# Three rounded products for mLSTM's scores, and moved loads and steps, in a two-layer trunk on one Trainium2 core

## The chip, the cores and the metric

The kernel runs on one core of a Trainium2 chip (trn2). The metric is device time in microseconds (us); the median of the runs counts. Before the change it is 1042.13 us (three runs, 1041.74 to 1042.76).

The engines are named as in the profile: PE is TensorE (matmuls; PEld is its loading of weights), DVE is VectorE, ACT is ScalarE, POOL is GpSimd, SP is SyncE. An engine's name with a q is its queue of instructions, from which it also issues DMAs.

## The reference

The trunk has two layers over 256 tokens of width 2048, all in float32. Layer 0 mixes with HGRN2 and RG-LRU side by side, layer 1 with mLSTM. Cut to what the change touches:

```python
hn = rmsnorm(h, o_norm)                      # layer 1
u = hn @ o_w_in
qk, v, og, z, ig, fg = split(u)              # fg, ig: 8 columns each, the gate columns
qk = silu(causal_conv(qk, c_conv_w, c_conv_b))
q, k = qk[..., :1024], qk[..., 1024:]        # 8 heads of 128
# per head, stabilised; wts holds the decays and gates, zero above the diagonal
sc = (q @ k.T) * wts
num = sc @ v ; den = sum(sc)
...
h = h + mix                                  # residual, in both layers
pl = rmsnorm(p[i] @ ple_w[i], ple_norm[i])   # embedding of the layer
h = h + sigmoid(h @ ple_gate_w[i]) * pl
```

## The kernel before

All large products are float32 products in three parts. `load_weights` (L120) loads 128 rows of weights as two tiles of 1024 columns, rounds each on ScalarE to `whi` (L132) and has VectorE subtract for the rest, `wlo` (L133). The activations are split in the same way into a high and a low part. A product is then hi x hi, hi x lo, lo x hi: L193, L194, L195 in `quarter_tok` (L182), 24 matmuls of 512 columns to a quarter (a fourth of the 2048 input rows, for two halves of the tokens), four quarters to a chunk of 512 output columns. The tiles `raw` have five buffers, `whi` and `wlo` four each. Results stand in PSUM tiles `mm` (three) and `mx` (three); the small products of the mixers use `mx` and `st`.

The small work of the mixers is written as generators. They sit in lanes, and `pump` (L75), once per quarter after its first twelve matmuls, takes one step of the first generator in each lane. A bare `yield` is thus a wait of one quarter. Work that goes from token-major to feature-major form makes a trip through DRAM (`across`, L449): VectorE transposes, GpSimd writes one DMA (L452) and reads it back with four (L455), and after `lag` quarters the next step uses what has landed. Within an engine the order is that of a scheduler, which weighs the written order, priorities and the availability it expects.

The places that the change touches:

- **Head.** `embed` (L272) multiplies the layer's input embedding with its weights, 48 products at L293. The first block's weights come in four pieces of 256 and two of 512 columns, the second block's first half in two pieces of 512. Two pieces go out on ScalarE's queue, all else on SyncE's. Nine full-precision warm-up products (L96) run before. L302 and L304 copy results out of PSUM.
- **Trips.** `feature_major` (L476) takes the gated HGRN2 output to feature-major form (scaling at L483, split at L146 and L147), with a lag of 5. `gated_mix` (L797) does so for the RG-LRU gate, with a lag of 6 for the first half and 5 for the second; L804 multiplies with the recurrence. RG-LRU's sigmoids are L775, its own products L151 to L153. L852 and L853 take the gate projection out of PSUM.
- **Residual.** The four tiles `hq` (512 KB each) are loaded back to back by GpSimd (L865) right after the last trip of layer 0; `out_proj` adds a chunk's product to each (L374). Two row loads for the embedding's gain (L322) follow once the mixer's memory is free; L329 reads them.
- **Gate columns.** Their weights `gr` (128 KB) are loaded by SyncE (L882) and scaled on VectorE to `wg` (L885); the gate sums use `wg` in small products (L896) from 467 us on.
- **Scores.** `mix` (L1011) treats two heads. For each head it multiplies keys and queries as full float32 products: the first 128 keys with 256 tokens (L1032), the other 128 keys with the last 128 tokens (L1033). L1018, L1019, L1023 and L1024 make the weights `wt` from the stabiliser, L1034 applies them, L1037 and L1038 split the result into `sh` and `sl`, and L1052 multiplies these with the values.

## Time and profile before

| | us |
|---|---|
| median of three runs | 1042.13 |
| the profiled execution's own time | 1042.44 |
| its span, first to last instruction | 1040.7 |
| TensorE busy (matmuls) | 1030.2 (99%) |
| VectorE busy | 730.4 (70%) |
| ScalarE busy | 601.7 (58%) |
| HBM traffic | 225 GB/s over the span |
| granted TensorE clock | 0.998 |

A row of the timeline gives the start, the duration, the engine and line, the operation with its tiles (out<-in), the shape, and how many like instructions were merged; in brackets stand the idle time of the engine before it and what ended that. A row of the waits gives who waited for whom, the sum, how often, and the longest. A row on DMA issues gives what is loaded, by which queue, how often, its size, and the time to landing. A matmul's row lasts from its start to its modelled end, which overlaps with the next one; the distance from start to start is what it costs.

### The profile page before, as it was taken

How to read it: one execution, taken by the hardware profiler on the slowest of the kernel's cores; microseconds unless marked ns; L12 is line 12 of the kernel's file. 1: busy time of each engine (PE TensorE's matmuls, PEld its weight loads, DVE VectorE, ACT ScalarE, POOL GpSimd, SP SyncE). 2: the span in 40 equal slices, each digit the busy share in tenths (PEclk: the TensorE clock that was granted, in tenths of full speed). 3: DMA queues.
4: the chain of work that ended last, by engine and by line, in shares of the span. 5: the costliest groups of instructions: out<-in, count | busy, mean ns of one | idle time of the engine just before them, and what ended most of it. 6: DMA issues, size and time to landing. Idle time of an engine off the chain costs nothing.

```text
span 1040.7 us, 14521 instructions
## 1 busy us (share of the span) xinstructions
PE 1030.2 (99%) x5278; PEld 854.7 (82%) x5278; DVE 730.4 (70%) x1101; ACT 601.7 (58%) x887; POOL 90.1 (9%) x171
## 2 busy tenths in 40 slices
PE   9999999999999999999999999999999999999996
PEld 7888888888888888888788788888888888888886
DVE  7858878969685775777569976555457777666675
ACT  7675555587974444565557765644445557344553
POOL 0111101001121211111021000000001110111000
PEclk9999999999999999999999999999999999999999
DMA  9977646567779877687587654455557778788552
GB/s 343 342 246 228 222 160 210 179 202 232 234 247 313 288 248 242 212 276 239 179 268 253 201 173 153 162 183 186 198 195 230 247 257 284 240 251 247 195 182 82
DMA packets 67752, 234.80 MB, mean 226 GB/s; under 512 B 8800, under 2 KB 10080, under 8 KB 67680
## 3 DMA queue, kind: packets, MB, share of 16 engines
q1 hardware_dynamic: 55728, 196.64, 56.9%
q0 software_dynamic: 11520, 36.71, 11.7%
q8 instruction: 41, 0.67, 0.3%
q10 hardware_dynamic: 432, 0.52, 0.1%
q14 instruction: 31, 0.25, 0.1%
HBM read 216.02 MB, written 17.83 MB: 225 GB/s over the span
## 4 chain that ended last, share of the span: by engine, by line
PE 91%; issue 4%; DMA 2%; ACT 1%; POOL 1%; DVE 0%; ACTq 0%; DVEq 0%; POOLq 0%; SPq 0%
PE mm L193 25%; PE mm L194 25%; PE mm L195 25%; PE mx L195 3%; PE mx L193 3%; PE mx L194 3%; PE mm L293 2%; DMA gr<-in_ogf_dram 1%; PE nu L1052 1%; DMA r<-dzb 1%; PE mm L1180 1%; PE mm L1179 1%; PE mm L1178 1%; DMA dzb<-w 1%; POOL r L455 1%
## 5 line engine op out<-in xcount | busy, mean ns | idle before, releaser
L133 DVE TENSOR_TENSOR wlo<-raw,whi 128x1024 fp32r<-128x1024 f32 (+2 forms) x365 | 437.7, 1207 | 228.7 <-ACT whi L132 215.9
L132 ACT CAST whi<-raw 128x1024 fp32r<-128x1024 f32 (+2 forms) x365 | 378.9, 1041 | 328.5 <-PE mm L195 260.0
L193 PE MATMUL mm<-whi,ahl 128*128 128x512 f32 x1216 | 475.6, 391 | 0.0
L194 PE MATMUL mm<-wlo,ahl 128*128 128x512 f32 x1216 | 473.8, 390 | 0.4 <-DVE wlo L133 0.4
L195 PE MATMUL mm<-whi,ahl 128*128 128x512 f32 x1216 | 473.3, 389 | 0.0
L193 PEld LDWEIGHTS mm<-whi,ahl 128*128 128x128 f32 x1216 | 228.3, 188 | 49.3 <-issue 1.2
L194 PEld LDWEIGHTS mm<-wlo,ahl 128*128 128x128 f32 x1216 | 228.3, 188 | 48.2 <-DVE wlo L133 2.0
L195 PEld LDWEIGHTS mm<-whi,ahl 128*128 128x128 f32 x1216 | 228.2, 188 | 47.8
L193 PE MATMUL mx<-whi,ahl 128*128 128x512 f32 x160 | 62.4, 390 | 0.0
L195 PE MATMUL mx<-whi,ahl 128*128 128x512 f32 x160 | 62.3, 389 | 0.0
L194 PE MATMUL mx<-wlo,ahl 128*128 128x512 f32 x160 | 62.3, 389 | 0.0
L195 PEld LDWEIGHTS mx<-whi,ahl 128*128 128x128 f32 x160 | 30.0, 188 | 6.3
L194 PEld LDWEIGHTS mx<-wlo,ahl 128*128 128x128 f32 x160 | 30.0, 188 | 6.3
L193 PEld LDWEIGHTS mx<-whi,ahl 128*128 128x128 f32 x160 | 30.0, 188 | 6.2
L452 POOL DMA_DIRECT2D ducn<-w x4 | 2.2, 560 | 221.4 <-DVE w L465 221.4
L944 DVE SCALAR_TENSOR_TENSOR qk<-xr,prm,qk 128x255 f32<-128x255 f32 (+2 forms) x48 | 20.3, 471 | 0.1
L147 DVE TENSOR_TENSOR ahl<-xr,ahl 128x512 fp32r<-128x512 f32 x24 | 16.3, 685 | 4.1 <-ACT ahl L146 4.0
L1179 PE MATMUL mm<-wlo,ahl 128*128 128x256 f32 x64 | 18.1, 283 | 0.0
L1180 PE MATMUL mm<-whi,ahl 128*128 128x256 f32 x64 | 18.1, 283 | 0.0
L1178 PE MATMUL mm<-whi,ahl 128*128 128x256 f32 x64 | 18.1, 283 | 0.0
L293 PE MATMUL mm<-whi,ahl 128*128 128x512 f32 x56 | 17.6, 391 | 0.0
L146 ACT CAST ahl<-xr 128x512 fp32r<-128x512 f32 x24 | 14.7, 612 | 4.0 <-DVE xr L804 3.9
(316 smaller groups left out, 811.6 us busy)
## 6 DMA issues: line engine op xcount, KB each, us to landing
raw<-in_ew_dram SPq DMA_DIRECT2D x64, 512.0 KB, 5.3
raw<-in_g_dram SPq DMA_DIRECT2D x56, 512.0 KB, 4.7
raw<-in_eo_dram SPq DMA_DIRECT2D x32, 512.0 KB, 6.0
raw<-in_oqk_dram SPq DMA_DIRECT2D x32, 512.0 KB, 4.8
raw<-in_ov_dram SPq DMA_DIRECT2D x32, 512.0 KB, 4.0
raw<-in_oog_dram SPq DMA_DIRECT2D x32, 512.0 KB, 3.9
raw<-in_oz_dram SPq DMA_DIRECT2D x32, 512.0 KB, 4.1
raw<-in_oo_dram SPq DMA_DIRECT2D x32, 512.0 KB, 4.9
```

Of the source, the lines that this page charges most:

```text
L132: last["act"] = s.copy(h, r).ins
L133: last["dve"] = v.tensor_tensor(out=l, in0=r, in1=h.bitcast(F32), op=ALU.subtract).ins
L146: (v.tensor_copy if name == "p0" else s.copy)(hi, src)
L147: v.tensor_tensor(out=lo, in0=src, in1=hi.bitcast(F32), op=ALU.subtract)
L193: te.matmul(ps[hf], xh, wh, start=(k == 0), stop=False)
L194: te.matmul(ps[hf], xh, wl, start=False, stop=False)
L195: last["pe"] = te.matmul(ps[hf], xl, wh, start=False, stop=(k == KT - 1)).ins
L293: last["pe"] = te.matmul(ps[hf], tokens(pact[x], k, hf), (hi, lo)[y][:, k * 512:(k + 1) * 512], start=(n == mine[0]), stop=(n == mine[-1]) ...
L944: v.scalar_tensor_tensor(dst[:, sh:T], pi[:, 0:T - sh], pc("ccw", k * 16 + n), dst[:, sh:T], op0=ALU.mult, op1=ALU.add)
L1178: te.matmul(ps[hf], xh, wh, start=(k == 0), stop=False)
L1179: te.matmul(ps[hf], xh, wl, start=False, stop=False)
L1180: last["pe"] = te.matmul(ps[hf], xl, wh, start=False, stop=(k == KT - 1)).ins
```

## The change

In the head, `load_weights` takes its queues in turn. The first block's pieces go out on ScalarE's and SyncE's queue alternately (three on each), and the second block comes as two loads of 1024 columns, like all later weights. The lag of the HGRN2 trips goes from 5 to 6 quarters, that of the second RG-LRU gate trip from 5 to 6. Only two residual tiles are loaded after the last trip; the third and fourth follow behind the trips of the first and second output chunks. The product that scales the gate columns is ordered behind the last weight subtraction written before it. The scores of the first 128 keys become three products of rounded parts; queries and those keys are split into parts one quarter ahead.

```diff
-    def load_weights(src, pieces=(1, 1), queues=8 * (sy,)):
+    def load_weights(src, pieces=(1, 1), queues=(sy,)):
...
-                queues[hf * 4 + c // n].dma_start(out=r, in_=src[:, hf * 1024 + c:hf * 1024 + c + n])
+                queues[c // n % len(queues)].dma_start(out=r, in_=src[:, hf * 1024 + c:hf * 1024 + c + n])
...
-            parts = load_weights(w[b], *((((4, 2), (s, s) + 6 * (sy,)) if head else ((2, 1),)) if first else ()))
+            parts = load_weights(w[b], *(((4, 2), (s, sy)) if head else ()))
...
-            r = yield from landed((u[:, 0], u[:, 1]), f"dzb{j}", 6 - j)
+            r = yield from landed((u[:, 0], u[:, 1]), f"dzb{j}", 6)
...
-                start(f"fm{g}", feature_major(u, "an", 4 * g, y, 5))
+                start(f"fm{g}", feature_major(u, "an", 4 * g, y, 6))
...
-    for i in range(4):
+
+    def load_hq(i, behind):
         t = hp.tile([P, 2, 512], F32, name="hq", tag="h")
-        with tc.issue_after(last["hop"]):
+        with tc.issue_after(behind):
             gp.dma_start(out=t, in_=a["x"].rearrange("(h p) f -> p h f", h=2)[:, :, i * 512:(i + 1) * 512])
         hq.append(t)
 
+    for i in range(2):
+        load_hq(i, last["hop"])
+
     def mixed():
         for c, ps in enumerate(chunks(a["eo"], 4, y, ready(y, "fm"))):
+            if c in (1, 2):
+                load_hq(c + 1, last["hop"])
...
-    v.tensor_tensor(out=wt[:, :, 0:16], in0=gr, in1=pall("on").unsqueeze(2).to_broadcast([P, KT, 16]), op=ALU.mult)
+    with tc.issue_after(last["dve"]):
+        v.tensor_tensor(out=wt[:, :, 0:16], in0=gr, in1=pall("on").unsqueeze(2).to_broadcast([P, KT, 16]), op=ALU.mult)
...
+        def room2(which):
+            return bp.tile([P, 1024], F32R, name=which, tag="wt")
+
...
             yield
-            yield
             while 4 + j not in qk:
                 yield
+            qhl = room2("qhl").rearrange("p (s i t) -> p s i t", s=2, i=2)
+            khl = tp.tile([P, 512], F32R, name="khl", tag="th").rearrange("p (s i t) -> p s i t", s=2, i=2)
+            for hl, src in ((qhl, qk[j].rearrange("p (i t) -> p i t", i=2)),
+                            (khl, qk[4 + j].rearrange("p (i t) -> p i t", i=2)[:, :, 0:P])):
+                s.copy(hl[:, 0], src)
+                v.tensor_tensor(out=hl[:, 1], in0=src, in1=hl[:, 0].bitcast(F32), op=ALU.subtract)
+            yield
             for i in range(2):
                 q, k = qk[j][:, i * T:(i + 1) * T], qk[4 + j][:, i * T:(i + 1) * T]
                 sc = px.tile([P, 512], F32, name="mx", tag="mx")
-                te.matmul(sc[:, 0:T], k[:, 0:P], q, start=True, stop=True)
+                for n, (x, z) in enumerate(((0, 0), (0, 1), (1, 0))):
+                    te.matmul(sc[:, 0:T], khl[:, x, i], qhl[:, z, i], start=(n == 0), stop=(n == 2))
                 te.matmul(sc[:, T:384], k[:, P:T], q[:, P:T], start=True, stop=True)
```

Three places show what moves in the engines' order. Line numbers in rows of the change are those of the changed kernel, 6 to 17 higher from L804 on. First VectorE around the gate columns' product, at 320 to 345 us; L133 is a weight subtraction, L804 and L147 make the last activations of the output projection, L329 reads the row loads, L374 adds the residual. Before:

```order
L133 TENSOR_TENSOR wlo<-raw,whi 128x1024 x4
L804 TENSOR_TENSOR xr<-r,tt 128x512 x2
L147 TENSOR_TENSOR ahl<-xr,ahl 128x2x256 x2
L133 TENSOR_TENSOR wlo<-raw,whi 128x1024 x2
L885 TENSOR_TENSOR wg<-gr,prm 128x16x16
L133 TENSOR_TENSOR wlo<-raw,whi 128x1024 x4
L329 TENSOR_TENSOR pl<-pl,row 128x512
L374 TENSOR_TENSOR hq<-mm,hq 128x512
```

And in the change:

```order
L133 TENSOR_TENSOR wlo<-raw,whi 128x1024 x6
L804 TENSOR_TENSOR xr<-r,tt 128x512 x2
L147 TENSOR_TENSOR ahl<-xr,ahl 128x2x256 x2
L133 TENSOR_TENSOR wlo<-raw,whi 128x1024 x4
L329 TENSOR_TENSOR pl<-pl,row 128x512
L374 TENSOR_TENSOR hq<-mm,hq 128x512
```

The product of the gate columns has left this place (it stands 56 instructions later), and L804 comes two subtractions later. Second, ScalarE ahead of the gate projection's way out of PSUM (L852, L853), at 280 to 293 us; L483 is the scaling of the second HGRN2 trip, L132 a weight cast, L782, L787 and L790 belong to RG-LRU. Before:

```order
L787 ACTIVATE sq<-av 128x512
L782 ACTIVATE av<-av,spm_242 128x256
L483 ACTIVATE xr<-r,prm 128x256
L787 ACTIVATE sq<-av 128x512
L852 ACTIVATE th<-mm,rth 128x512
L853 ACTIVATE u<-mm,rcr 128x512
```

And in the change:

```order
L787 ACTIVATE sq<-av 128x512
L782 ACTIVATE av<-av,spm_239 128x256
L787 ACTIVATE sq<-av 128x512
L852 ACTIVATE th<-mm,rth 128x512
L853 ACTIVATE u<-mm,rcr 128x512
L852 ACTIVATE th<-mm,rth 128x512
L853 ACTIVATE u<-mm,rcr 128x512
L790 ACT_TABLE_LOAD
L790 ACTIVATE tt<-tt 128x1024
L132 CAST whi<-raw 128x1024 x3
L483 ACTIVATE xr<-r,prm 128x256
```

The scaling has moved behind both pairs of copies, the square root and three casts. Third, VectorE ahead of the first score weighting (L1034 before, L1051 now), at 597 to 606 us; L944, now L951, is a tap of the convolution of the last queries and keys, L948, now L955, closes it. Before:

```order
L944 SCALAR_TENSOR_TENSOR qk<-xr,prm,qk 128x255 x2
L948 SCALAR_TENSOR_TENSOR qk<-th,qk 128x512
L944 SCALAR_TENSOR_TENSOR qk<-xr,prm,qk 128x254 x2
L944 SCALAR_TENSOR_TENSOR qk<-xr,prm,qk 128x253
L133 TENSOR_TENSOR wlo<-raw,whi 128x1024 x2
L944 SCALAR_TENSOR_TENSOR qk<-xr,prm,qk 128x253
L1034 SCALAR_TENSOR_TENSOR wt<-mx,wt 128x384
```

And in the change:

```order
L1043 TENSOR_TENSOR qhl<-qk,qhl 128x512
L951 SCALAR_TENSOR_TENSOR qk<-xr,prm,qk 128x255
L955 SCALAR_TENSOR_TENSOR qk<-th,qk 128x512
L1043 TENSOR_TENSOR khl<-qk,khl 128x256
L951 SCALAR_TENSOR_TENSOR qk<-xr,prm,qk 128x254
L133 TENSOR_TENSOR wlo<-raw,whi 128x1024
L951 SCALAR_TENSOR_TENSOR qk<-xr,prm,qk 128x253
L133 TENSOR_TENSOR wlo<-raw,whi 128x1024
L951 SCALAR_TENSOR_TENSOR qk<-xr,prm,qk 128x255
L951 SCALAR_TENSOR_TENSOR qk<-xr,prm,qk 128x254
L1051 SCALAR_TENSOR_TENSOR wt<-mx,wt 128x384
```

The two subtractions of the split (L1043) stand ahead of the last two weight subtractions before the scores are weighted.

## The prediction

> **What bounds the kernel now.** I read the page's busy line first, then TensorE's own waits, then its timeline for the pace of the matmuls. Row by row: start in us, duration, instruction, how many were merged, and in brackets the idle time before it and what ended it.
>
> ```profile
> PE 1030.2 (99%) x5278; PEld 854.7 (82%) x5278; DVE 730.4 (70%) x1101; ACT 601.7 (58%) x887; POOL 90.1 (9%) x171
> PE mm L194 <- DVE wlo L133: 0.4, 1, 0.4
> ACT whi L132 <- PE mm L195: 260.0, 218, 4.3
> 20.04 0.39 PE L195 MATMUL mm<-whi,ahl 128*128 128x512 f32 x1
> ...
> 22.54 0.39 PE L194 MATMUL mm<-wlo,ahl 128*128 128x512 f32 x1
> ...
> 29.11 0.62 PE L193 MATMUL mm<-whi,ahl 128*128 128x512 f32 x2
> ```
>
> TensorE is busy 99% of the span and VectorE 70%. Once its products run, TensorE is seen idle for VectorE once, for 0.4 us; ScalarE's weight casts waited 218 times for TensorE to free a buffer. So TensorE sets the time. But a matmul's row is 0.39 long while the next starts sooner, so busy time hides small losses; the pace shows them. From 20.04 to 29.11 there are 40 starts: 0.2268 us each. Looking over all starts for steps longer than their kind's usual one, and leaving out those that come back at every small product, five places stand out: the head (0 to 22.5 us), 260.7, 268.2, 283.6 and 333.7. Elsewhere weight parts are ready early: with four buffers, one is freed 18 products into its quarter and its next part is needed 30 products later, 6.8 us, of which cast and subtraction take 1.05 and 1.23 (rows below): 4.5 us in hand. So the change can win only by less TensorE work or at these places, and can lose wherever it makes an operand late. The whole is a matter of about 2 us in 1042.
>
> **Head.**
>
> ```profile
> 3.60 1.70 PE L96 MATMUL st<-ones 128*128 128x128 f32 x7
> 5.34 2.12 PE L293 MATMUL mx<-whi,ahl 128*128 128x512 f32 x8
> 4.36 1.54 ACT L132 CAST whi<-raw 128x256 fp32r<-128x256 f32 x4 [1.42 <-DMA raw<-in_pw_dram]
> ...
> 8.36 0.62 ACT L132 CAST whi<-raw 128x512 fp32r<-128x512 f32 x1 [0.55 <-DMA raw<-in_pw_dram]
> ...
> 9.84 0.63 ACT L132 CAST whi<-raw 128x512 fp32r<-128x512 f32 x1
> 10.79 1.05 ACT L132 CAST whi<-raw 128x1024 fp32r<-128x1024 f32 x1 [0.33 <-DMA raw<-in_pw_dram]
> 11.88 1.23 DVE L133 TENSOR_TENSOR wlo<-raw,whi 128x1024 fp32r<-128x1024 f32 x1 [0.68 <-ACT whi L132]
> ```
>
> From the first product at 5.34 to the L194 at 22.54 lie 48 embedding products, 24 of the first quarter and one more: 73 steps. At 0.2268 they need 16.55 us, and they took 17.20, so 0.65 is lost. Two edits act here. First, the second 256-column piece goes out on SyncE's queue instead of as the second issue of ScalarE's, so pieces arrive in the order in which they are cast. The last warm-up product is over at about 5.1 (seven in the row, 0.21 apart), and the product starts at 5.34 after the second cast; I take 0.15 us (bounds 0 and 0.25). Second, the first 1024 columns of the second block come as one load, with one cast and one subtraction, instead of two halves. Their casts stood at 8.36 and 9.84, so the whole tile is there between these times. Add 1.05 (cast) and 1.23 (subtraction): the low part is ready between 10.6 and 12.1. The product that needs it would start at 5.2 + 25 x 0.2268 + 0.1 = 11.0. So this edit costs between nothing and 1.2 us with the slow restart seen at each stall (0.1). I take an arrival at 8.9 and 0.3 us. In exchange, the copy that frees a PSUM tile no longer queues behind late casts, and the loads behind, with fewer and longer lines, come no later. Of the 0.65 lost I keep 0.05 beside the 0.3. Head: -0.15 - 0.65 + 0.35 = **-0.45** (from -0.8 to +0.4).
>
> The Trainium skill, "DMA: Bandwidth & Descriptors", section "Issuing engines are not separate DMA queues", says that DMAs of all issuers share the same 16 engines, and that several issuers save only the time of issuing. By that rule the queue edit gives at most the issue itself; at nothing, the forecast would be 0.15 us higher. No row of before separates the two.
>
> **The gate columns' product.**
>
> ```profile
> 332.82 0.43 DVE L885 TENSOR_TENSOR wg<-gr,prm 128x256 f32<-128x256 f32 x1 [7.46 <-DMA gr<-in_ogf_dram]
> 333.16 4.62 DVE L133 TENSOR_TENSOR wlo<-raw,whi 128x1024 fp32r<-128x1024 f32 x4
> 337.70 0.68 DVE L329 TENSOR_TENSOR pl<-pl,row 128x512 f32<-128x512 f32 x1
> 333.69 0.39 PE L193 MATMUL mm<-whi,ahl 128*128 128x512 f32 x1
> 334.44 0.50 PE L194 MATMUL mm<-wlo,ahl 128*128 128x512 f32 x1 [0.36 <-DVE wlo L133]
> 334.77 0.39 PE L195 MATMUL mm<-whi,ahl 128*128 128x512 f32 x1
> hq<-in_x_dram POOLq DMA_DIRECT2D x4, 512.0 KB, 11.9
> ...
> row<-in_rows_dram POOLq DMA_DIRECT2D x2, 512.0 KB, 10.5
> ...
> gr<-in_ogf_dram SPq DMA_DIRECT2D x1, 128.0 KB, 11.5
> ```
>
> VectorE stood 7.46 us before L885, waiting for a 128 KB load that took 11.5 us behind four residual loads of 512 KB. Four weight subtractions were queued behind it, and TensorE ran dry: steps of 0.75 and 0.33 instead of 0.227, a loss of 0.52 + 0.11 = 0.63. In the change the product stands after later subtractions, well after the load, and its reader (the gate sums) comes over 100 us later. The four subtractions follow their casts. Gain **-0.63**. What is late next: the two row loads, since their memory comes free only after L804, which now stands two subtractions later. They are read at L329, which ran at 337.7. With 10.5 us from some 327 they land at about 337.5, so the cover is nearly used up. A landing up to 4 us later still costs nothing, since weight parts have 4.5 us in hand there; beyond that, up to the 0.63 again. The third and fourth residual loads go out after later trips on GpSimd's queue, each 0.7 us of issue ahead of the next trip. By 11.9 us per load they land before their sums, one chunk (96 products, 21.8 us) after issue. I cost them at nothing.
>
> **Trips one step later.**
>
> ```profile
> 281.70 0.50 ACT L483 ACTIVATE xr<-r,prm 128x256 f32<-128x256 f32 x1
> ...
> 283.19 0.68 ACT L853 ACTIVATE u<-mm,rcr 128x512 f32<-128x512 f32 x1
> 283.59 0.39 PE L195 MATMUL mm<-whi,ahl 128*128 128x512 f32 x1
> 283.92 0.50 PE L193 MATMUL mm<-whi,ahl 128*128 128x512 f32 x1
> 284.25 0.40 PE L194 MATMUL mm<-wlo,ahl 128*128 128x512 f32 x1
> 260.73 0.39 PE L193 MATMUL mm<-whi,ahl 128*128 128x512 f32 x1
> 261.21 0.50 PE L194 MATMUL mm<-wlo,ahl 128*128 128x512 f32 x1
> ```
>
> At 283.9 TensorE takes a PSUM tile that L853 frees at 283.87: steps of 0.33 and 0.34, 0.2 lost. The first scaling L483 moves behind three weight casts, so L853 ends about 0.4 earlier: **-0.2** (bounds 0 and -0.2). At 261.2 the step is 0.48 for the product that reads a low part, 0.25 too long, and 0.1 follows; the order ahead of that subtraction on VectorE hardly changes, so I leave the loss there (bounds 0 and -0.4, with some 0.05 at 268.2).
>
> **The scores.**
>
> ```profile
> 603.64 0.59 PE L1032 MATMUL mx<-qk 128*128 128x256 f32 x2
> 604.07 0.38 PE L1033 MATMUL mx<-qk 128*128 128x128 f32 x2
> 611.39 0.29 PE L1052 MATMUL nu<-vl,sh 128*128 128x256 f32 x1
> 611.51 0.28 PE L1052 MATMUL nu<-vt,sh 128*128 128x258 f32 x1
> L1052 PEld LDWEIGHTS nu<-vt,sh x24: 187/188/193, 610.2 to 673.6; 128*128 128x128 f32 x24
> 593.45 0.51 ACT L1023 ACTIVATE wt<-wt,aT 128x256 f32<-128x256 f32 x1 [1.58 <-DVE wt L1018]
> 604.49 0.56 DVE L1034 SCALAR_TENSOR_TENSOR wt<-mx,wt 128x384 f32<-128x384 f32 x1 [0.67 <-PE mx L1033]
> L147 DVE TENSOR_TENSOR ahl<-xr,ahl 128x512 fp32r<-128x512 f32 x24 | 16.3, 685 | 4.1 <-ACT ahl L146 4.0
> L146 ACT CAST ahl<-xr 128x512 fp32r<-128x512 f32 x24 | 14.7, 612 | 4.0 <-DVE xr L804 3.9
> ```
>
> One full-precision product over 256 columns takes 0.43 us (603.64 to 604.07). Rounded products of that width follow each other at 0.12 (611.39 to 611.51), so three take 0.36. Eight heads: 8 x -0.07 = **-0.55**. Per pair of heads this adds a cast and a subtraction of 128x512 (0.61 and 0.69) and one of each of 128x256, about 0.4 us each: some 1.0 us on ScalarE and 1.1 on VectorE, four times. They stand one quarter (24 products, 5.4 us) ahead of the products, and ScalarE was idle for 1.58 ahead of the first exponentials. VectorE had only 0.67 us idle ahead of the first L1034, so there the score weighting starts some 0.4 us later; the weight loads of the products that read it begin at 610.2, over 5 us after it. I cost them at nothing.
>
> A weight load lasts 0.188 us, longer than a rounded product's step. The Trainium skill, "TensorE: Matmul & The Clock Gate", section "Back-to-back issue gap", says that the spacing is set by load and matmul together. Were the load to bind here, three products would take 0.56 instead of 0.36, and the edit would cost 8 x 0.13 = 1.0 us. The L1052 rows, with the same loads at 0.12 per step, speak against it.
>
> **Sum.** -0.45 - 0.63 - 0.2 - 0.55 = -1.83. The profiled execution took 1042.44 (span 1040.7 and 1.74 around it), so 1040.6 by its measure; the median of the runs is 0.31 lower, which gives **1040.3**.
>
> **Rivals.** (1) *More goes.* The stall at 261 goes too and the head loses nothing: -0.8 - 0.63 - 0.2 - 0.4 - 0.57 = -2.6, 1039.5. For it: the same engines are relieved; against it: nothing ahead of that subtraction changes. (2) *One late big load.* The 512 KB tile lands at 9.84: head +0.4, so 1041.1. (3) *Row loads take the gate load's place* and stall VectorE at L329: 1040.9. This is also the case in which the rescheduling doesn't do what it says. (4) *Weight loads bind the scores*: 1040.3 + 1.6 = 1041.9. (5) *Slower*: the rounded parts come late. If ScalarE and VectorE are more than 3.4 us behind when the splitting starts (5.4 less its 2 us), TensorE waits at all four pairs for up to the 2.1 us of the split: 4 x 2.1 = 8.4 on top of the rest, 1040.3 + 8.4 = 1048.7. Against it: the idle times above, and weight parts 4.5 us ahead, which leave both engines room to do the split first.
>
> **How the numbers follow.** Forecast (1039.8 to 1040.9) 0.46, rivals 0.25, 0.12, 0.08, 0.04 and 0.05. The range 1039.4 to 1042.0 takes in all but (5) and some scatter. A measurement here can tell about 0.2%, or 2.1 us: faster than 1040.05 is (1) and a quarter of the forecast, 0.36; slower is (5), 0.05; the rest, 0.59, is no change.
>
> **What would show it.** L885's successor without idle before it; steps of 0.227 at 333.7 and 283.9; the 73 steps of the head in under 17 us; three products of the scores in 0.36 instead of 0.43, and no wait of TensorE on the new parts. A wait of VectorE at L329 on the rows, or of TensorE at about 11 us, would make it wrong.

## The result, and the profile after

The changed kernel takes 1040.81 us (median of 21 runs, 1040.48 to 1041.18), the kernel before 1042.13 us in the same session (21 runs, 1041.45 to 1043.40): a ratio of 0.9985, 95% interval 0.998 to 0.9991. That is 1.3 us faster, and by the bound of 0.2% that the prediction set itself no change. The profiled execution took 1040.62 us, its span 1038.8 us. (Up to L861 the lines of both kernels have the same numbers; behind it those of the changed kernel are up to 17 higher.)

The busy line of the page reads as before; TensorE still sets the time:

```profile
PE 1029.3 (99%) x5286; PEld 855.1 (82%) x5286; DVE 734.3 (71%) x1108; ACT 604.1 (58%) x894; POOL 90.3 (9%) x171
```

To see where the time went, cut TensorE's stream at three marks: the first small product of the attention (L601), the first gate sum (L896 before, L903 after) and the last product. From the timeline of the kernel before, first profile:

```profile
95.84 0.89 PE L601 MATMUL mx<-q,k 128*32 128x48 f32 x64
...
467.72 1.07 PE L896 MATMUL mx<-r,wg 128*32 128x256 f32 x16
...
1031.54 0.28 PE L1180 MATMUL mm<-whi,ahl 128*128 128x256 f32 x1
```

From the timeline of the changed kernel:

```profile
95.95 0.89 PE L601 MATMUL mx<-q,k 128*32 128x48 f32 x64
...
467.12 1.07 PE L903 MATMUL mx<-r,wg 128*32 128x256 f32 x16
...
1030.19 0.28 PE L1197 MATMUL mm<-whi,ahl 128*128 128x256 f32 x1
```

The pieces between the marks, with the last one up to the end of the span, are these in all fourteen profiles (kernels that are explained below):

| kernel | head, to L601 | to the gate sum | to the last product | tail |
|---|---|---|---|---|
| before | 95.84 | 371.88 | 563.82 | 9.13 |
| **changed** | 95.95 | 371.17 | 563.07 | 8.66 |
| before, profiled again | 96.61 | 371.28 | 563.82 | 9.13 |
| before + head loads | 96.61 | 371.22 | 563.82 | 9.19 |
| changed, old head | 96.18 | 371.17 | 563.07 | 8.61 |
| before + gate edit, two profiles | 96.27, 96.15 | 371.27, 371.28 | 563.82, 563.82 | 9.12, 9.14 |
| before + lags, two profiles | 96.26, 96.04 | 371.16, 371.25 | 563.82, 563.82 | 9.13, 9.14 |
| before + scores | 96.72 | 371.22 | 563.07 | 8.59 |
| changed, fourth piece alone | 96.15 | 371.16 | 563.07 | 8.64 |
| changed, no cover for the split | 96.22 | 371.15 | 563.33 | 8.67 |
| changed, all scores rounded | 96.05 | 371.22 | 564.54 | 8.66 |
| changed, two places mended | 96.11 | 370.55 | 563.07 | 8.66 |

Between the two first profiles the differences are +0.11, -0.71, -0.75 and -0.47, in all -1.82. Read down the columns, though, and they are not of one kind. The third and fourth are the same to 0.1 us in every kernel with the same code there. The first moves by 0.9 us over all, and by 0.77 us between two profiles of one kernel already. And 371.88 stands there once, in the first profile of before, and never again.

Now the places of the prediction. **Scores**, first the large product behind the first pair of heads in the kernel before, then the timeline of the changed kernel:

```profile
604.86 0.48 PE L193 MATMUL mm<-whi,ahl 128*128 128x512 f32 x1
```

```profile
603.03 0.52 PE L1049 MATMUL mx<-qhl,khl 128*128 128x256 f32 x3
603.39 0.38 PE L1050 MATMUL mx<-qk 128*128 128x128 f32 x2
603.53 0.60 PE L1049 MATMUL mx<-qhl,khl 128*128 128x256 f32 x3
603.83 0.55 DVE L1051 SCALAR_TENSOR_TENSOR wt<-mx,wt 128x384 f32<-128x384 f32 x1
603.97 0.38 PE L1050 MATMUL mx<-qk 128*128 128x128 f32 x2
604.11 0.48 PE L193 MATMUL mm<-whi,ahl 128*128 128x512 f32 x1
```

Three rounded products take 0.36 us (603.03 to 603.39). From the first product of the pair to the first large product behind it are 1.08 us; before, from 603.64 (shown in the prediction) to 604.86, there were 1.22. In TensorE's waits the rounded parts do not occur.

**Gate columns**, VectorE's timeline of the changed kernel, where before VectorE had stood idle for 7.46 us ahead of L885:

```profile
328.28 2.58 DVE L133 TENSOR_TENSOR wlo<-raw,whi 128x1024 fp32r<-128x1024 f32 x2 [0.31 <-ACT whi L132]
333.72 2.59 DVE L133 TENSOR_TENSOR wlo<-raw,whi 128x1024 fp32r<-128x1024 f32 x2 [2.85 <-ACT whi L132]
336.22 0.69 DVE L329 TENSOR_TENSOR pl<-pl,row 128x512 f32<-128x512 f32 x1
```

The subtractions follow their casts, and L329 finds its rows (no idle time ahead of it). **Trips**, timeline of the changed kernel:

```profile
283.00 0.68 ACT L853 ACTIVATE u<-mm,rcr 128x512 f32<-128x512 f32 x1
...
283.42 0.39 PE L194 MATMUL mm<-wlo,ahl 128*128 128x512 f32 x1
...
283.73 0.50 PE L193 MATMUL mm<-whi,ahl 128*128 128x512 f32 x1
284.06 0.40 PE L194 MATMUL mm<-wlo,ahl 128*128 128x512 f32 x1
```

L853 ends at 283.68 instead of 283.87, early enough for the product in its old place (due at 283.87 in this stream), and still there are steps of 0.31 and 0.33: 0.19 us lost instead of 0.21. Look at the operation ahead of the waiting L193. Before it was L195, now it is L194: the product that takes the freed tile has moved one place forward. **Head**, ScalarE's timeline of the changed kernel (casts of the pieces), then TensorE's:

```profile
4.25 1.09 ACT L132 CAST whi<-raw 128x256 fp32r<-128x256 f32 x3 [0.82 <-DMA raw<-in_pw_dram]
6.26 0.41 ACT L132 CAST whi<-raw 128x256 fp32r<-128x256 f32 x1 [0.92 <-DMA raw<-in_pw_dram]
6.86 1.26 ACT L132 CAST whi<-raw 128x512 fp32r<-128x512 f32 x2 [0.19 <-DMA raw<-in_pw_dram]
9.18 1.05 ACT L132 CAST whi<-raw 128x1024 fp32r<-128x1024 f32 x1 [1.07 <-DMA raw<-in_pw_dram]
```

```profile
5.08 2.83 PE L293 MATMUL mx<-whi,ahl 128*128 128x512 f32 x8
```

Three pieces are early; the fourth is cast at 6.26 after a wait for its DMA, where before all four were done by 5.90. And eight products fill a row of 2.83 us where they filled one of 2.12 before: the first start in steps of 0.59, 0.43, 0.43 and 0.28. The 73 steps of the head took 17.57 us instead of 17.20, and 0.84 of the 1.01 us lost (73 x 0.2268 = 16.56) lies in the first five. **Tail**, ScalarE's timeline, before and then changed (the queue's row is the issue of a store):

```profile
1035.25 0.38 ACTq L1225 DMA_DIRECT2D out_dram<-pl  x1
1035.95 0.51 ACT L1217 ACTIVATE pl<-pl,fr 128x256 f32<-128x256 f32 x1 [0.73 <-ACT pl L1220]
```

```profile
1033.90 0.37 ACTq L1242 DMA_DIRECT2D out_dram<-pl  x1
1034.32 0.51 ACT L1234 ACTIVATE pl<-pl,fr 128x256 f32<-128x256 f32 x1 [0.45 <-ACT pl L1237]
```

ScalarE's last operation starts 0.05 us behind the end of its issue instead of 0.32. The store that waits for it goes out 4.76 us after the last product (4.95 before) and has landed at 7.56 instead of 8.09 us after it. So only 0.19 of the 0.53 us is there at its issue; the rest comes on the way. It shows better in the store before it, which both kernels issue 4.24 us after the last product. Its issue and time to landing, and a load of instructions (8 KB, one packet) in the DMA queues; first before (windows of 1035.7 to 1036.0 and 1037.2 to 1037.6 us), then changed (1034.4 to 1034.6 and 1027.0 to 1027.6):

```profile
out_dram<-pl SPq DMA_DIRECT2D x1, 256.0 KB, 3.3
q14 instruction: 1, 0.01, 4.8%
```

```profile
out_dram<-pl SPq DMA_DIRECT2D x1, 256.0 KB, 2.9
q14 instruction: 1, 0.01, 5.5%
```

In the kernel before the instructions are loaded 5.87 us after the last product, among the last stores; in the changed kernel they had come 2.96 us ahead of it.

### The profile page after: what moved, and what is told of

Read it like the earlier page. It is cut to its first block, busy times and chain, and to the rows that moved or that the text cites. A ratio compares the mean times of both kernels' runs of the same rounds, so it can differ in the third digit from the quotient of the medians.

```text
span 1038.8 us, 14550 instructions
## 1 busy us (share of the span) xinstructions
PE 1029.3 (99%) x5286; PEld 855.1 (82%) x5286; DVE 734.3 (71%) x1108; ACT 604.1 (58%) x894; POOL 90.3 (9%) x171
## 4 chain that ended last, share of the span: by engine, by line
PE 95%; DVE 2%; ACT 2%; issue 1%; ACTq 0%; POOL 0%; DVEq 0%; POOLq 0%
PE mm L193 26%; PE mm L194 25%; PE mm L195 25%; PE mx L195 3%; PE mx L193 3%; PE mx L194 3%; PE mm L293 2%; DVE wlo L133 1%; PE nu L1069 1%; PE mm L1197 1%; PE mm L1196 1%; PE mm L1195 1%; ACT whi L132 1%; PE mx L601 0%; DVE xc L812 0%
## 5 line engine op out<-in xcount | busy, mean ns | idle before, releaser
L133 DVE TENSOR_TENSOR wlo<-raw,whi 128x1024 fp32r<-128x1024 f32 (+1 forms) x364 | 437.7, 1210 | 233.6 <-ACT whi L132 220.9
L132 ACT CAST whi<-raw 128x1024 fp32r<-128x1024 f32 (+1 forms) x364 | 378.6, 1044 | 327.8 <-PE mm L195 260.1
L193 PE MATMUL mm<-whi,ahl 128*128 128x512 f32 x1216 | 475.7, 391 | 0.0
L194 PE MATMUL mm<-wlo,ahl 128*128 128x512 f32 x1216 | 473.3, 389 | 0.1
L195 PE MATMUL mm<-whi,ahl 128*128 128x512 f32 x1216 | 472.9, 389 | 0.0
L193 PEld LDWEIGHTS mm<-whi,ahl 128*128 128x128 f32 x1216 | 228.3, 188 | 49.0 <-issue 1.2
L195 PEld LDWEIGHTS mm<-whi,ahl 128*128 128x128 f32 x1216 | 228.2, 188 | 47.9
L194 PEld LDWEIGHTS mm<-wlo,ahl 128*128 128x128 f32 x1216 | 228.3, 188 | 47.2 <-DVE wlo L133 0.7
L193 PE MATMUL mx<-whi,ahl 128*128 128x512 f32 x160 | 62.4, 390 | 0.0
L195 PE MATMUL mx<-whi,ahl 128*128 128x512 f32 x160 | 62.3, 389 | 0.0
L194 PE MATMUL mx<-wlo,ahl 128*128 128x512 f32 x160 | 62.3, 389 | 0.0
L195 PEld LDWEIGHTS mx<-whi,ahl 128*128 128x128 f32 x160 | 30.0, 188 | 6.3
L194 PEld LDWEIGHTS mx<-wlo,ahl 128*128 128x128 f32 x160 | 30.0, 188 | 6.3
L193 PEld LDWEIGHTS mx<-whi,ahl 128*128 128x128 f32 x160 | 30.0, 188 | 6.2
L951 DVE SCALAR_TENSOR_TENSOR qk<-xr,prm,qk 128x255 f32<-128x255 f32 (+2 forms) x48 | 20.6, 471 | 0.1
L147 DVE TENSOR_TENSOR ahl<-xr,ahl 128x512 fp32r<-128x512 f32 x24 | 16.3, 686 | 4.0 <-ACT ahl L146 3.9
```

What stands on the lines that cost most here:

```text
L132: last["act"] = s.copy(h, r).ins
L133: last["dve"] = v.tensor_tensor(out=l, in0=r, in1=h.bitcast(F32), op=ALU.subtract).ins
L147: v.tensor_tensor(out=lo, in0=src, in1=hi.bitcast(F32), op=ALU.subtract)
L193: te.matmul(ps[hf], xh, wh, start=(k == 0), stop=False)
L194: te.matmul(ps[hf], xh, wl, start=False, stop=False)
L195: last["pe"] = te.matmul(ps[hf], xl, wh, start=False, stop=(k == KT - 1)).ins
```

## The experiments

### The head: three orders of loads

**Head loads alone.** The kernel before, with

```diff
-    def load_weights(src, pieces=(1, 1), queues=8 * (sy,)):
+    def load_weights(src, pieces=(1, 1), queues=(sy,)):
...
-                queues[hf * 4 + c // n].dma_start(out=r, in_=src[:, hf * 1024 + c:hf * 1024 + c + n])
+                queues[c // n % len(queues)].dma_start(out=r, in_=src[:, hf * 1024 + c:hf * 1024 + c + n])
...
-            parts = load_weights(w[b], *((((4, 2), (s, s) + 6 * (sy,)) if head else ((2, 1),)) if first else ()))
+            parts = load_weights(w[b], *(((4, 2), (s, sy)) if head else ()))
```

> The kernel before with the change's head loads alone. What happens in the head is read from the stream's first product behind it that starts a recurrent small product (L601, at 95.62 us in the trace of before, 95.73 in that of the change). Theory P (the prediction's step): the pieces arrive in the order in which they are used, 0.45 us is gained, so L601 at about 95.2 and the time 0.45 us lower. Theory Q (two queues issue at once): the fourth piece of 256 columns is issued at the same moment as the first of 512 on the other queue, lands at about 6.2 us instead of 5.2, and the fifth product cannot start before 6.7 (6.38 before); L601 at about 95.7, time 0 to 0.3 us higher. Theory R (pace of TensorE): the first products run at 0.43 us each until TensorE quickens, at a moment that differs from run to run and has nothing to do with the change; then L601 stands anywhere from 95.2 to 96.2, and the fourth piece's landing does not decide.

(The two places that this text gives for L601 are those of the product just ahead plus a tenth; its own row starts 0.22 us later, at 95.84 and 95.95. Add 0.22 to the other places too.)

Measured: 1041.95 us (11 runs) against 1042.22 (21 runs), ratio 0.9999, interval 0.9991 to 1.0008; L601 at 96.61. ScalarE's timeline of this kernel:

```profile
4.11 1.08 ACT L132 CAST whi<-raw 128x256 fp32r<-128x256 f32 x3 [0.69 <-DMA raw<-in_pw_dram]
7.07 1.45 ACT L132 CAST whi<-raw 128x256 fp32r<-128x256 f32 x3 [1.88 <-DMA raw<-in_pw_dram]
```

Here the fourth piece came at 7.05, 1.9 us after the third was cast, and the fifth product started at 7.53. So the step that P rests on did not come, and L601 stands no earlier. The time alone does not exclude P: 0.45 us less would be a ratio of 0.9996, which lies in the interval.

**Old head.** The changed kernel with these three edits undone.

> The changed kernel with the head loads of before, all else as changed. Theory P: 0.45 us is lost, 1041.3 us. Theory Q: the fourth piece lands at about 5.2 us, L601 at about 95.5 to 95.6 and the time up to 0.3 us lower than the change's, 1040.5 to 1040.8. Theory R: the place of L601 follows the moment at which weight loads of TensorE fall from 0.33 to 0.19 us, and the median differs by less than 0.2 us in either direction.

Measured: 1040.80 us (11 runs), against 1040.81 for the changed kernel in another session; ratio to before 0.9988 (0.9979 to 0.9997); L601 at 96.18. ScalarE's last three casts of 256 columns stand in one row from 4.81 to 5.83. P's 1041.3 was not measured, though as a ratio (0.9991) it lies in this interval, too.

**The fourth piece by itself.** The changed kernel with

```diff
-                queues[c // n % len(queues)].dma_start(out=r, in_=src[:, hf * 1024 + c:hf * 1024 + c + n])
+                (sy if hf else queues[c // n % len(queues)]).dma_start(out=r, in_=src[:, hf * 1024 + c:hf * 1024 + c + n])
```

> The changed kernel with one thing more in the head: only the four pieces of 256 columns alternate between the two queues, the two of 512 go out on SyncE's queue alone, so that nothing is issued together with the fourth piece. Theory Q (two queues issue at once): the fourth piece lands at about 5.2 us instead of 6.2 (7.05 in the run of the head loads alone), the fifth product starts at 6.4 or earlier unless TensorE is still slow, the first L193 at about 16.5 instead of 16.9, and the median is 0.2 to 0.5 us lower than the change's 1040.81. Theory R (pace of TensorE alone): the piece lands early, but the products wait for nothing and run at 0.43 us each until TensorE quickens; the median moves by less than 0.15 us.

Measured: 1040.89 us (11 runs), ratio to before 0.9985 (0.9976 to 0.9993). ScalarE's timeline of this kernel has all four casts in one row:

```profile
4.42 1.34 ACT L132 CAST whi<-raw 128x256 fp32r<-128x256 f32 x4 [1.48 <-DMA raw<-in_pw_dram]
```

So the mechanism of Q is shown: with nothing issued beside it the fourth piece lands at 5.27; issued in the same moment as a 512-column piece on the other queue it landed between 6.11 and 7.05 in five profiles. But no time came of it. The first four products ran in steps of 0.59, 0.43, 0.41 and 0.23, and the fifth began at 6.86 although its operand had been there for a microsecond. That is R. TensorE's weight loads show it best; each row or pair of rows has the loads of the first eight products. First the kernel before, first profile; then the same kernel, profiled again; then the changed kernel:

```profile
5.34 1.69 PEld L293 LDWEIGHTS mx<-whi,ahl 128*128 128x128 f32 x8 [0.33 <-ACT whi L132]
```

```profile
5.34 2.52 PEld L293 LDWEIGHTS mx<-whi,ahl 128*128 128x128 f32 x8 [0.32 <-ACT whi L132]
```

```profile
5.08 1.35 PEld L293 LDWEIGHTS mx<-whi,ahl 128*128 128x128 f32 x4
6.71 0.76 PEld L293 LDWEIGHTS mx<-whi,ahl 128*128 128x128 f32 x4 [0.28 <-ACT whi L132]
```

One load lasts 0.29 to 0.33 us while TensorE is slow (0.33 in the warm-up products ahead) and 0.19 when it is quick. In the first profile of before all were quick; in the second, of the same code, five of eight were slow, and in the changed kernel four of eight. Over fourteen profiles TensorE was quick at the first product in four, after one or two products in three, after three or four in five, after about five in two. The warm-up products start at 1.10 in all of them, so TensorE quickened no later than 4.2 us after its first product in one execution and no sooner than 6.0 us in another. The Trainium skill, "TensorE: Matmul & The Clock Gate", section "Part 1: The HAM clock gate (the "warmup" mystery)", says that TensorE runs at half its clock until it has been busy for one free-running window of about 3.4 us, so that the moment depends on where in a window the first product falls. By that page it would come 3.4 to 6.8 us after the first product (an estimate from its window); the halved pace, 4.2 and 6.0 us, and a moment that changes between two executions of one kernel agree with it; the 4 us give or take 0.5 that the same section reports as observed do not cover 6.0. That it is the clock, these runs do not show: the granted clock reads 1.00 from 0 to 8 us both in the first profile of before and in the changed kernel, quick or slow. What the runs do not settle either: of eight profiles with the old head seven quickened before the third product, of the six others none did before the fourth. Whether the order of the loads has a part in that, or chance, stays open.

With the old head another place loses instead. The last 1024-column tile lands at 11.1 to 11.6 us in six of eight profiles (10.2 to 10.7 in five with the new head), and a product at about 12.8 starts 0.3 to 0.6 us late in five of them. ScalarE's timeline of the run with the scores alone, which has the old head, tells why:

```profile
11.25 1.05 ACT L132 CAST whi<-raw 128x1024 fp32r<-128x1024 f32 x1 [0.89 <-DMA raw<-in_pw_dram]
12.20 1.06 ACT L304 COPY pl<-mm 128x512 f32<-128x512 f32 x2
```

and TensorE's waits of the same run:

```profile
PE mm L293 <- ACT pl L304: 0.4, 1, 0.4
```

The copy that frees a PSUM tile is queued behind a cast that waits for its DMA. With the new head the low part of the single large tile comes late instead, by 0.03 us in the profile of the changed kernel, by 0.24 to 0.28 in three others and not at all in two. Means over eight profiles with the old head and five with the new one tell where it goes: the first product starts 0.27 us earlier with the new head (5.02 instead of 5.29), the first five steps lose 0.80 us more (1.12 instead of 0.32), and the 68 steps behind them lose 0.59 less (0.19 instead of 0.78). L601 stands at 96.26 with the old head and at 96.19 with the new one. The head edits move where TensorE waits and are worth nothing that these runs can tell.

### The stall at 333.7: gate columns and lags

**Gate edit alone**, profiled in one execution and later timed in more. The kernel before, with

```diff
-    v.tensor_tensor(out=wt[:, :, 0:16], in0=gr, in1=pall("on").unsqueeze(2).to_broadcast([P, KT, 16]), op=ALU.mult)
+    with tc.issue_after(last["dve"]):
+        v.tensor_tensor(out=wt[:, :, 0:16], in0=gr, in1=pall("on").unsqueeze(2).to_broadcast([P, KT, 16]), op=ALU.mult)
```

> The kernel before with nothing but the product of the gate columns ordered behind the last weight subtraction; the four residual loads stay together. Theory P: the steps of 0.75 and 0.33 us at 333.7 become 0.227, and the first gate sum (467.6 us before) stands 0.63 us earlier relative to the products ahead of the stall; the edit of the residual loads is not needed for it. Rival: the 128 KB load and the two row loads stay behind the four residual loads, VectorE then waits at L329 or the stall is moved, and less than 0.3 us of it goes.

> The gate columns' product alone once more, timed. Theory F: the median is 0.6 us lower than that of before. Theory L: the stall stands in a part of the executions only, so the median falls by 0.1 to 0.4 us, and the spread between the lowest and the highest run shrinks.

Measured: in both profiles the steps at 333.7 are 0.227, and L601 to the gate sum takes 371.27 and 371.28, 0.6 less than in the first profile of before. So P looked right. But the time did not follow: 1042.26 us in the first execution, then 1042.17 us (11 runs) against 1042.24 (21 runs), ratio 1.0, interval 0.9991 to 1.0009 (0.6 us less would be 0.9994, so the time alone does not exclude F). The scatter did not shrink either (1041.54 to 1043.56).

**Before, once more.**

> The kernel before, unchanged, profiled once more. Theory L (the stall at 333.7 hangs on the 128 KB load's landing in that execution): the load lands 9 to 11 us after issue and VectorE has its product done before TensorE needs the next low part, so the steps of 0.75 and 0.33 us are absent or shorter, as in the runs of the head loads alone and of the scores alone, which share this code. Theory F (a fixed cost): 0.63 us stands there as in the first profile. In the head the new trace gives one more place of the first L193 (16.59 us in the first profile of before, 16.98 to 17.06 in three later kernels with the same head): if 16.6 was a lucky execution, it is about 17.0.

Measured: 1042.61 us in one execution, L601 to the gate sum 371.28: no stall, in the very kernel in which it had been found. VectorE's timeline of this profile:

```profile
331.78 0.42 DVE L885 TENSOR_TENSOR wg<-gr,prm 128x256 f32<-128x256 f32 x1 [5.58 <-DMA gr<-in_ogf_dram]
332.12 4.91 DVE L133 TENSOR_TENSOR wlo<-raw,whi 128x1024 fp32r<-128x1024 f32 x4
```

VectorE waits for the 128 KB load as before, but the load lands at 331.69, 9.7 us after its issue, and not at 332.73, 11.5 us after it. The stream was 0.77 us later (L601 at 96.61 instead of 95.84), so the low part was needed 0.8 us later too. 1.0 us earlier here and 0.8 later there: the wait is over before TensorE asks. The runs of the head alone and of the scores alone share this code; their loads took 9.4 and 9.9 us, and there was no stall. So F is out and L holds: of four profiles that share this code one had the stall, and taking it away is worth 0.07 us in the median, which is nothing that can be told.

**Lags alone**, profiled in one execution and later timed in more:

```diff
-            r = yield from landed((u[:, 0], u[:, 1]), f"dzb{j}", 6 - j)
+            r = yield from landed((u[:, 0], u[:, 1]), f"dzb{j}", 6)
...
-                start(f"fm{g}", feature_major(u, "an", 4 * g, y, 5))
+                start(f"fm{g}", feature_major(u, "an", 4 * g, y, 6))
```

> The kernel before with the two lags of the trips alone. Theory P: L853 ends about 0.2 to 0.4 us earlier and the loss of 0.21 us at 283.6 goes. Theory S (the order of TensorE moves along): L853 ends 0.2 us earlier, but the scheduler lets the product that takes the freed PSUM tile go one product sooner, as it does in the change, so TensorE waits one product earlier for nearly as long: 0.0 to 0.05 us gained at 283.6, and 0.06 at 268.2.

> The two lags alone once more, timed. In the first look at it the gate columns' load went out 5.2 us later (its place in the queue moved with the trips), landed 4.3 us after issue, and the stall at 333.7 was gone with the old order of the gate columns' product. Theory T (the lags alone do the gate edit's work): the median falls by 0.07 us for the trips and by as much as the gate edit alone for the stall. Theory P (the lags are worth 0.2 us at 283.9 and nothing at 333.7): the median falls by 0.2 and the stall at 333.7 is there in the new trace.

Measured: 1042.14 us in the first execution; 1042.09 us (11 runs) against 1042.24 when timed, ratio 0.9999 (0.999 to 1.0008). At 283.7 the loss is 0.21 us in both, with L194 ahead of the waiting L193: S is right, the gain at 283 is nothing. And the stall at 333.7 is absent in both although L885 stands in its old place: with the lags the gate columns' load goes out at 326.9 instead of 321.2 and lands 4.3 and 4.4 us later, so VectorE starts the product at 331.3 after an idle time of 0.2 and 0.3 us and is done with it at 331.8, ahead of the 332.2 that made no stall in the second profile of before. That speaks for T: where the stall does occur, the lags would take it away, and the gate edit is not needed beside them. It is argued from the landings; in two profiles the stall could also have been absent by chance.

### Two places mended

The changed kernel with two edges that only set an order:

```diff
+    waits = {}
...
+                if waits.get("t"):
+                    waits["t"][1] -= 1
+                    if not waits["t"][1]:
+                        tc.add_manual_dep(waits.pop("t")[0], last["dve"].name, mybir.DependencyInfo(
+                            mybir.DependencyClass.NoSync, mybir.DependencyReason.DATA), reason="order")
...
-                te.matmul(ps[hf], xh, wh, start=(k == 0), stop=False)
+                m = te.matmul(ps[hf], xh, wh, start=(k == 0), stop=False).ins
...
+                if w is a["ew"] and j == 7:
+                    if hf == 1 and k == 0:
+                        waits["m"] = m
+                    if hf == 0 and k == 7:
+                        tc.add_manual_dep(waits["m"], last["pe"].name, mybir.DependencyInfo(
+                            mybir.DependencyClass.NoSync, mybir.DependencyReason.DATA), reason="order")
...
-            v.transpose(w5[:, hf], u[hf].rearrange("p (c j q) -> p c j q", c=4, j=4))
+            t = v.transpose(w5[:, hf], u[hf].rearrange("p (c j q) -> p c j q", c=4, j=4)).ins
+        if name == "duan4":
+            waits["t"] = [t, 2]
```

> The changed kernel with two edges that set an order and nothing else: the product that takes the freed PSUM tile at 283 us goes behind the last L195 of the tile before it, and the transpose of the second HGRN2 trip's second half goes behind the weight subtraction that TensorE waits for at 261 us. Theory S (at 283 the scheduler let the product move along with its tile): the loss of 0.19 us at 283.4 goes, since L853 ends at 283.68 and the product is due at 283.88. At 261 the subtraction starts at 259.46 instead of 260.09 and ends before it is needed at 261.08, so 0.36 us goes. Together 0.55 us, median about 1040.3. Rival (both are waits for something else, or the time is lost at the next place): less than 0.2 us.

Measured: 1040.15 us (11 runs) against 1042.35 for before, ratio 0.9979 (0.997 to 0.9988). The changed kernel with the fourth piece alone, in the same session, took 1040.89, and the changed kernel itself 1040.81 in another; so this version is some 0.7 us faster than the change. L601 to the gate sum falls by 0.62 us, from 371.17 to 370.55. Timeline of this kernel at both places (its lines are 1 to 14 higher: L134 is the weight subtraction, L477 the transpose, L199 to L201 the products, L867 the copy that frees the tile):

```profile
259.61 1.23 DVE L134 TENSOR_TENSOR wlo<-raw,whi 128x1024 fp32r<-128x1024 f32 x1
...
260.76 0.70 DVE L477 STREAM_TRANSPOSE w<-u 128x512 f32<-128x512 f32 x1
...
261.00 0.39 PE L199 MATMUL mm<-whi,ahl 128*128 128x512 f32 x1
261.23 0.39 PE L200 MATMUL mm<-wlo,ahl 128*128 128x512 f32 x1
```

```profile
282.76 0.68 ACT L867 ACTIVATE u<-mm,rcr 128x512 f32<-128x512 f32 x1
...
283.41 0.39 PE L201 MATMUL mm<-whi,ahl 128*128 128x512 f32 x1
...
283.64 0.39 PE L199 MATMUL mm<-whi,ahl 128*128 128x512 f32 x1
```

Both places now run in steps of 0.23. At 283 the copy was no earlier in its place than in the changed kernel (it ends 0.20 us ahead of the L199 that needs it); what had failed there was TensorE's order alone.

### The scores

**Scores alone**: the kernel before with the change's edits of `mix` and nothing else.

> The kernel before with the scores' three rounded products alone. Theory P (the prediction's step): 8 x 0.07 = 0.55 us less between 590 and 675 us, no wait of TensorE on the rounded parts. Rival (weight loads bind): three products take 0.56 us instead of 0.43, 1.0 us more. The trace of the change shows 0.18 us less per pair of heads, so 0.7 in all, if nothing else in the change helps there. The same run tells something of the stall at 333.7, whose code it shares with the kernel before: if the stall is a fixed cost (theory F), the steps 0.75 and 0.33 stand there again; if it hangs on how long the 128 KB load takes in an execution (theory L; 11.5 us in the trace of before, 9.4 in that of the head loads alone, where the stall was absent), it is there only when that load takes over about 11 us.

Measured: 1041.37 us in one execution; gate sum to last product 563.07, 0.75 less than before, as in every kernel that has the change's scores as they are; no wait on the rounded parts; no stall at 333.7. P's mechanism is right and its size too small. The tail is 8.59: the 0.5 us there comes with this edit too, in all seven profiles that have it and in none of the other seven.

**No cover.** The changed kernel with the split in the same step as the products:

```diff
                 s.copy(hl[:, 0], src)
                 v.tensor_tensor(out=hl[:, 1], in0=src, in1=hl[:, 0].bitcast(F32), op=ALU.subtract)
-            yield
             for i in range(2):
```

> The changed kernel with the split of queries and keys in the same step as the products that use the parts, so that the quarter of cover is gone. Theory P (the cover is what hides the split): TensorE waits at each of the four pairs for up to 2.1 us, 2 to 8.4 us in all. Rival (the engines have room and the scheduler places the products behind the split by itself): under 0.5 us in all, and the products only stand some steps later in TensorE's order.

Measured: 1041.14 us in one execution; gate sum to last product 563.33, 0.26 more than in the changed kernel, and TensorE's waits show none on the parts. P (2 to 8.4 us) falls: the scheduler found other work for TensorE while the parts were made. In the first pair it laid two large products between those of the scores; in the second, five rounded products of both heads stand in a row instead of three of one; in the third and fourth the last part was ready 3.8 us ahead of the products. The quarter of distance, on which the prediction rested the price of nothing, is worth 0.3 us.

**All scores rounded.** The changed kernel, with

```diff
-            khl = tp.tile([P, 512], F32R, name="khl", tag="th").rearrange("p (s i t) -> p s i t", s=2, i=2)
+            khl = room2("khl").rearrange("p (s i t) -> p s i t", s=2, i=2)
...
-                            (khl, qk[4 + j].rearrange("p (i t) -> p i t", i=2)[:, :, 0:P])):
+                            (khl, qk[4 + j].rearrange("p (i t) -> p i t", i=2))):
...
-                    te.matmul(sc[:, 0:T], khl[:, x, i], qhl[:, z, i], start=(n == 0), stop=(n == 2))
-                te.matmul(sc[:, T:384], k[:, P:T], q[:, P:T], start=True, stop=True)
+                    te.matmul(sc[:, 0:T], khl[:, x, i, 0:P], qhl[:, z, i], start=(n == 0), stop=(n == 2))
+                for n, (x, z) in enumerate(((0, 0), (0, 1), (1, 0))):
+                    te.matmul(sc[:, T:384], khl[:, x, i, P:T], qhl[:, z, i, P:T], start=(n == 0), stop=(n == 2))
```

> The changed kernel with the other product of the scores (128 keys with 128 tokens) made of three rounded products as well; all 256 keys are split, so ScalarE's cast and VectorE's subtraction of the keys cover 128x512 instead of 128x256. In full precision this product takes 0.22 us (two records 0.11 apart). Theory N (paced by columns): a rounded product over 128 columns takes 0.06 us, three take 0.18 and eight heads gain 0.3 us. Theory W (a weight load that hides behind 256 columns does not hide behind 128): a step of 0.1 us or more each, three take 0.3 or more, and eight heads lose 0.7 us or more.

Measured: 1042.24 us in one execution; gate sum to last product 564.54, 1.47 more. A pair of heads takes 1.32 us instead of 1.08 (0.24 more, 0.96 in four pairs); 0.46 of the other 0.51 is one wait for a result tile at 672.4. TensorE's weight loads in this kernel:

```profile
602.96 0.53 PEld L1049 LDWEIGHTS mx<-qhl,khl 128*128 128x128 f32 x3
603.41 0.42 PEld L1051 LDWEIGHTS mx<-qhl,khl 128*128 128x128 f32 x3
603.75 0.42 PEld L1049 LDWEIGHTS mx<-qhl,khl 128*128 128x128 f32 x3
```

The three loads for the products over 128 columns, up to the next load, take 0.34 us (603.41 to 603.75): 0.11 apart, though each is recorded as 0.19. W holds for the time. Is it the load that binds, or has a product over 128 columns a floor of its own? Small full-precision products of the kernel before speak for the load; they stream 8 columns only but load 128:

```profile
591.21 0.61 PE L1001 MATMUL mx<-cst,li 8*128 8x8 f32 x4
591.67 0.59 PE L1001 MATMUL mx<-cst,Bc 8*128 8x8 f32 x4
```

Four starts take 0.46 us (591.21 to 591.67), again 0.11 to 0.12 each. So the pace of 0.11 does not come from the columns that are streamed. Loads overlap; a product over 256 columns (0.12) hides one, a product over 128 columns does not. The Trainium skill, "TensorE: Matmul & The Clock Gate", section "LDWEIGHTS (loading the stationary operand)", gives 1/1.2 ns per column, which makes 107 ns for 128 (an estimate from that formula); the 0.11 agrees, and the 0.19 of the records is not what binds.

## Why the prediction was right and wrong

The forecast was 1040.3 us, in a range of 1039.4 to 1042.0; 1040.81 lies in it. Between the two first profiles even the sum agrees: -1.83 forecast, -1.82 measured. That is chance. Step by step:

- **Head, -0.45: wrong.** +0.11 between the two profiles, -0.01 us in the median when it is undone. The first product started 0.26 us earlier (0.15 forecast), and the pieces do land in the order in which they are cast. The step that failed is the loss that was to remain, 0.35: the 73 steps took 17.57 us (under 17 was to show it) and lost 1.01, 0.84 of it in the first five. The sum had no term for TensorE being slow there, which it is until 5 to 7 us, and took it that no piece would land later for the new order; but the fourth shares its way with a larger piece that another queue issues in the same moment. Even when that piece comes early nothing is won. The 0.3 taken for the single large load was about its largest cost (0.03 there, 0.24 to 0.28 in three other profiles, none in two). The base was unlucky as well: the first profile of before has the earliest L601 of all fourteen.
- **Gate columns, -0.63: right for that execution, wrong as a term.** The step that failed is that a stall seen in one profiled execution was counted in full for all. It hung on a load that took 11.5 us there and 9.4 to 9.9 in three others. In the median it is 0.07 us.
- **Trips, -0.2: wrong.** L853 ended 0.19 us earlier, 0.24 against the stream around it (0.4 was expected), and that would have been enough. The step that failed is "L853 ends earlier, so the loss goes": the scheduler moved the product that waits for it forward by one place, 0.23 us. Mending only the order brought it. Some 0.05 us at 268.2 came, as had been put down for it.
- **Scores, -0.55: right in mechanism, too small.** -0.75. The three products take the 0.36 that was forecast, and a pair of heads needs 1.08 us instead of 1.22 (-0.14, as 2 x -0.07; -0.57 in four pairs). The other 0.18, some 0.04 to 0.05 a pair, lies in the large products behind them, in steps that are up to 0.01 us shorter than before; why is open.
- **Not forecast at all: the tail, -0.47.** It comes with the scores' edit. ScalarE's last operation starts 0.27 us sooner behind its own issue, with no wait shown ahead of it in either kernel, and the last stores land sooner after their issue. In all seven profiles without this edit one load of instructions falls among these stores (5.87 to 5.89 us after the last product); in all seven with it, it comes 2.6 to 3.0 us ahead of the last product. That fits an edit that adds instructions and so moves the place at which the next ones are loaded; no run tested it, so the cause stays open.
- **Costed at nothing: right.** No wait on the rounded parts, none at L329, none for the third and fourth residual load. But the reason given for the parts, a quarter of distance, carries only 0.26 us of it.

Rival (4), weight loads that bind, is out for 256 columns and real for 128. Rivals (2), (3) and (5) did not occur, and neither did (1), since the stall at 261 stayed until an edge of its own took it.

In sum, then: 0.75 and 0.5 us from the scores and about 0.1 from the lags by the columns of the table, nothing that can be told from head and gate edit by the medians. That makes 1.35, and 1.32 were measured (0.9 to 2.1 by the interval, so that so close an agreement is in part luck). Head and gate edit fell some 1.0 us short of their terms, trips 0.1; the scores and the tail gave 0.7 us more than theirs.

## What to carry to other kernels

A stall that ends with a DMA's landing can be a draw and not a cost, as at 333.7: profile the same kernel a second time before it is put into a sum. When a release comes earlier, see what the scheduler does with the instruction that waits for it, since it may move along and keep the stall. And compare kernels between marks in the stream: a column that repeats to 0.1 us over many kernels tells more than a median whose runs scatter by one or two.

## What the runs showed of the hardware

- Two queues that issue in the same moment can share the way: the fourth piece, 128 KB, landed 3.4 to 3.6 us after its issue where nothing was issued with it, and 4.5 to 5.4 us after it where another queue issued a 256 KB piece in the same moment (1.64 and 1.66 us in the changed kernel). Two pieces of 128 KB that were issued together half a microsecond earlier (1.18 us) show no such delay: 3.3 to 3.8 us.
- The same 128 KB load behind four 512 KB loads took 9.3 to 11.5 us over six executions; issued 5 us later it took 3.2 to 5.0 over eight (4.3 and 4.4 in the two with all four residual loads still together).
- TensorE's moment of quickening differs by at least 1.8 us between two executions of one kernel: no later than 5.34 us (first weight load of 0.19) in the first profile of before, no sooner than 7.12 (end of a load of 0.33) in the second.
- Weight loads of 128 columns follow each other at 0.11 us, though each is recorded as 0.19, and the products go at that pace whether they stream 128 columns or 8.
- One 8 KB load of instructions among the last stores goes with landings of the last three on SyncE's queue that are 0.2 to 0.5 us later (seven profiles with it, seven without).
